# A float32 encoder on one Trainium2 core: the six split-weight buffers at six addresses modulo 256 bytes

## The chip, the core and the metric

The kernel runs on one core of one Trainium2 chip. The metric is the device time of one execution in microseconds (us). Everything is float32; each matrix product is computed from operands that are split into a high and a low part, so one product becomes three matrix instructions.

## What is computed

Two layers of a streaming encoder over 512 frames of width 1024 (batch 1), and a final norm. Cut to what matters here:

```python
h = rmsnorm(x, norm1_g[i])
z = h @ w_in[i] + b_in[i]                  # 1024 -> 12296 columns
# branch A: 4-head mLSTM on conv + silu of q, k; branch B: 4-head retention on rotary q, k
merged = sigmoid(gm) * (y_m @ w_bm[i]) + sigmoid(gr) * (y_r @ w_br[i])
x = x + merged @ w_out[i]
h2 = rmsnorm(x, norm2_g[i])
x = x + square(relu(h2 @ w_ff1[i] + b_ff1[i])) @ w_ff2[i] + b_ff2[i]
h3 = rmsnorm(x, norm3_g[i])
x = x + sigmoid(h3 @ w_pe_gate[i]) * (p[i] @ w_pe[i])
...
return rmsnorm(x, final_g)
```

## The kernel before

Activations lie transposed in the core's memory (features in the 128 partitions, 512 frames along the row), weights come from device memory in the order of a list of units. A **unit** is a 1024 x 128 column block (T8: eight 128 x 128 pieces), a value block (V), a PAIR (two such column blocks, multiplied by a seven-product scheme with halves of the operands) or a WIDE (the same scheme with 512 weight columns moving). For every 1024-column piece of a unit, `prep_next` takes the raw tile `wr` that a load on SP's queue has filled and splits it: ScalarE copies it rounded into `wh` (L303), VectorE subtracts and writes the rest into `wl` (L304). TensorE then runs, for each 128 x 128 piece, three instructions: weight high x activation high, weight high x activation low, weight low x activation high (`mm3`, L480 to L482; in pairs L531 to L533 with 256 columns moving; in WIDE units L575 to L577, where a piece of the activation sits still and 512 weight columns move). GpSimd's queue adds weight pieces in device memory ahead of time for the seven-product scheme (L361).

TensorE's work is written out in program order, and VectorE's and ScalarE's splits are held in the order of the units. `unit` and `ready` keep the splits two pieces ahead of TensorE; six buffers of 1024 columns (tag "w", three pieces of a high and a low tile) and two of 512 columns (tag "d") hold the split weights. The pools stand one behind the other from the low end of the 128 rows: constants, columns, a filler of 48 floats (`pad`), the weight pool (`wr` four buffers, "w" six, "d" two), then the tiles that live through the kernel, then pools that come and go by phase, on the left (low addresses) or on the right (from the top).

All sizes but the small ones are multiples of 256 bytes, so what decides an address modulo 256 is the filler and a small tile named `shift`. In the program before, every weight buffer, raw or split, starts at 224 modulo 256. So do all the activation tiles that TensorE reads, but for three groups that a `shift` tile of 16 floats moves to 32: the operand sums of the seven-product scheme in the first half of a layer (`xsh`, `xsl`), the hidden tiles of the feed-forward (`hh`, `hl`) and the embedding input (`pth`, `ptl`). The operands `xnh`, `xnl`, `ymh`, `yrh`, `n2h`, `nsh`, `nsl` and the like are at 224.

```python
    def shift(pl, side, start):

        if (side == "left") == start:
            pl.tile([P, 16 if start else 48], F32, name="shift", tag="shift")
```

Of the kernel before, what the change touches and what calls it, by code (L numbers as in the profile page):

```python
# [35 lines left out]
F32 = mybir.dt.float32  # L36
F32R = mybir.dt.float32r
# [5 lines left out]
P = 128  # L43
# [4 lines left out]
L = 2  # L48
# [8 lines left out]
NTMP = 6  # L57
RAWS = 4
PIECES = 3
PAD = 48  # L60
LAST = 4
SIGN = (1.0, -1.0)

# [60 lines left out]
def is_wide(g):  # L124
    return g[1][:2] in ("rv", "rw")
# [7 lines left out]
def has_t2(g):  # L133

    return is_full(g) or g[1][0] == "f"
# [117 lines left out]
def build(ctx, tc, ins, out):  # L253
# [3 lines left out]
    NU = len(units)  # L257

    def pool(name, bufs, **kw):
        return ctx.enter_context(tc.tile_pool(name=name, bufs=bufs, **kw))  # L260
# [3 lines left out]

    cpool = pool("const", 1)
    cols = pool("cols", 2)
    padp = pool("pad", 1)
    padp.tile([P, PAD], F32, name="pad")
    wpool = pool("w", PIECES)
    bpool = pool("big", 1)  # L270
    opool = pool("one", 1)
# [30 lines left out]
    def split(src, hi_ap, lo_ap):  # L302
        a = ac.activation(hi_ap, src, AF.Copy)  # L303
        return a, ve.tensor_sub(lo_ap, src, hi_ap.bitcast(F32))  # L304

    def in_order(kind, *new):

        for a, b in zip(cur.get(kind, ()), new):
            tc.add_manual_dep(b.ins, a.ins.name, ORDER, reason="order of the weights")
        cur[kind] = new  # L310
# [4 lines left out]
    for g, v in groups().items():  # L315
        index[g] = len(index)
        src, n, w = ("wwide", 2, UN) if is_wide(g) else ("wpairs", len(v), Q)
# [63 lines left out]
    def full(n):  # L381
        return units[n][0] in ("PAIR", "WIDE") and is_full(units[n][1])
# [10 lines left out]
    def halves(n):  # L393

        return [slice(0, Q), slice(Q, UN)] if n == 1 else [slice(0, UN)]

    def fill_raws(most=RAWS + 1):
        while at["load"] < len(loads) and len(raws) + len(kept) < most:
            n, x = loads[at["load"]]
            r = None  # L400
            if n in cur["room"] and cur["more"] not in raws:
                cur["more"] = n, x
                r = cur["low"].tile([P, UN], F32, name=f"wr{at['load']}", tag="wrx", bufs=1)
            elif len(raws) - (cur["more"] in raws) >= RAWS:
                break
            raws[n, x] = r = r or wpool.tile([P, UN], F32, name=f"wr{at['load']}", tag="wr", bufs=RAWS)
            if x:
                _, g, p = units[n]
                assert made.get((g, x[1] if is_wide(g) else p)) == 2 * len(MADE_OF(g)), (g, p, made, at["unit"])
                if is_wide(g):  # L410
                    in_order("load", nc.sync.dma_start(r, block(g, x[0])[x[1]]))
                else:
                    for k, y in enumerate(PIECE[x][:1] if x == "B" and not has_t2(g) else PIECE[x]):
                        in_order("load", nc.sync.dma_start(r[:, k * Q:(k + 1) * Q], block(g, y)[p]))
            elif units[n][0] == "IF":
                eng = nc.sync if n else nc.scalar
                eng.dma_start(r[:, 0:64], ins["wif"][n * L // NU])
            else:
                w = ins["wstream"][at["whole"]]
                for c in halves(n):  # L420
                    in_order("load", nc.sync.dma_start(r[:, c], w[:, c]))
                at["whole"] += 1
            at["load"] += 1

    def prep_next():
        n, x = order[at["prep"]]
        at["prep"] += 1
        fill_raws()

        w = Q if x == "D" else UN  # L430
        pl = cur["last"] if n >= NU - LAST else wpool
        kw = {"tag": "d", "bufs": 2} if x == "D" else {"tag": "l", "bufs": 2 * LAST} if pl is not wpool else {
            "tag": "w", "bufs": 2 * PIECES}
        wide = isinstance(x, tuple)
        nm = f"{x[0]}{x[1]}" if wide else x
        gates = units[n][0] == "IF"
        out_ = [pl.tile([P, w], F32R, name=f"w{a}{n}_{nm}", **kw) for a in ("h" if gates else "hl")]
        r = formed.pop((n, x), None)
        if r is None:
            r = raws.pop((n, x))  # L440
        if gates:
            z = out_[0]
            gp.memset(z.bitcast(F32), 0.0)
            z = z.rearrange("p (k g c) -> p k g c", g=4, c=32)
            split(r[:, 0:64].rearrange("p (k g c) -> p k g c", g=2, c=H), z[:, :, 0:2, 0:H], z[:, :, 2:4, 0:H])
        elif x == 0:
            with tc.high_priority(AHEAD if n < 10 and units[n][0] == "V" or units[n][1:] == SOON else 0):
                for c in halves(n):
                    in_order("prep", *split(r[:, c], *[a[:, c] for a in out_]))
        else:  # L450
            in_order("prep", *split(r[:, :w], *out_))
        pieces[n, x] = out_
        if full(n) or not wide and x in ("A", "C") and has_t2(units[n][1]):
            pass
        elif x == "A" or wide and x[0] == "t2":
            kept[n, x] = r
        elif x == "C":

            ve.tensor_tensor(raws[n, "B"][:, Q:], kept.pop((n, "A"))[:, Q:], r[:, :Q], OP.add)
        elif x == "B":  # L460

            ve.tensor_tensor(r[:, :Q], r[:, :Q], r[:, Q:], OP.add)  # L462
            formed[n, "D"] = r
        elif wide and x[0] == "B21":
            t = cur["br"].tile([P, UN], F32, name=f"t4{n}_{x[1]}", tag=("ph", "pl")[x[1]])
            ve.tensor_tensor(t, kept.pop((n, ("t2", x[1]))), r, OP.add)
            formed[n, ("t4", x[1])] = t

    def ready(k):
        while at["prep"] < min(len(order), k + 1):  # L470
            prep_next()

    def unit(kind):
        n = next_unit()
        assert units[n][0] == kind, (units[n], kind)
        ready(place[n, 0] + LOOK)
        return units[n], *pieces.pop((n, 0))
# [497 lines left out]
    for i in range(L):  # L975
# [34 lines left out]
        _, wi = unit("IF")  # L1010
        _, wh, wl = unit("T8")
        og = ps(f"l{i}if")
        oz = ps(f"l{i}m0z0")
        for k in range(KT):
            s = slice(k * P, (k + 1) * P)
            f, e = k == 0, k == KT - 1
# [281 lines left out]
        for d in range(4):  # L1298
# [8 lines left out]
            a = (f"l{i}m0{d}", 8 * (d // 2) + d % 2, qk[2 * (d // 2)][d % 2], qk[2 * (d // 2) + 1][d % 2], d < 2, n1)  # L1307
# [347 lines left out]
    for a, n in enumerate(nn):  # L1655
        for c in range(KT - LAST, KT):
            _, wh, wl = ws[c - KT + LAST]
# [143 lines left out]
```

## Time and profile before

| what | value |
|---|---|
| time, median of 2 runs | 2318.26 us (2317.53 to 2318.99) |
| span of the profiled execution | 2313.4 us, first to last instruction |
| outside the span, by the median | 4.9 us |
| TensorE matmul busy | 2299.1 us (99%), 13532 instructions |
| TensorE weight load busy | 2035.4 us (88%) |
| VectorE, ScalarE, GpSimd busy | 1766.8, 1269.6, 624.1 us |
| mean granted TensorE clock | 0.998 |

A row of the timeline gives the start in us, the duration in us, the engine (PE is TensorE, DVE VectorE, ACT ScalarE, POOL GpSimd), the line, the operation, output<-inputs, and the shape. A matmul's duration contains its way through the array and overlaps the next one, so its cost in a stream is the distance from its start to the next start. PEld is TensorE loading the next 128 x 128 piece that sits still, beside the running matmul.

### The profile page before, as it was taken

Reading aid. Unit: us, or ns where it says so; the run is one execution under the profiler, and the core shown is the slowest. Engines: PE = TensorE matmul, PEld = TensorE weight load, DVE = VectorE, ACT = ScalarE, POOL = GpSimd, SP = SyncE. Lnnn points to the kernel's source line nnn. Section 1 sums busy time; section 2 is a strip of 40 time slices with the busy share of each in tenths; the row PEclk is TensorE's granted clock in tenths of the full one; section 3 lists DMA queues with packets and bytes.
Section 4 is the critical chain, followed back from the end, with each engine's and each line's share of the span. In section 5 each row is a group of like instructions: output and inputs, shape, how many; then the busy total and the mean of one; then the engine's idle time right before and its main releaser. Section 6 shows DMA issues by size and latency. Waiting matters only on the chain.

```text
span 2313.4 us, 36468 instructions
## 1 busy us (share of the span) xinstructions
PE 2299.1 (99%) x13532; PEld 2035.4 (88%) x13532; DVE 1766.8 (76%) x2690; ACT 1269.6 (55%) x1837; POOL 624.1 (27%) x984
## 2 busy tenths in 40 slices
PE   9999999999999999999999999999999999999998
PEld 8888899888898899999888888988888888999997
DVE  7878767886676878788778777778867678787785
ACT  6756544644554546556557564445445446566564
POOL 4333222223124322223442332221231242111112
PEclk9999999999999999999999999999999999999999
DMA  7776787777789888888886768877877898878851
GB/s 218 189 191 174 238 228 216 215 227 210 232 230 261 220 228 223 240 239 215 222 224 182 196 174 247 232 216 216 223 221 208 241 266 218 247 232 228 232 160 55
DMA packets 187603, 499.36 MB, mean 216 GB/s; under 512 B 26064, under 2 KB 29520, under 8 KB 187424
## 3 DMA queue, kind: packets, MB, share of 16 engines
q0 software_dynamic: 57520, 188.53, 37.1%
q1 hardware_dynamic: 114496, 281.06, 36.6%
q10 hardware_dynamic: 15408, 27.43, 3.5%
q8 instruction: 106, 1.74, 0.3%
q14 instruction: 73, 0.60, 0.1%
HBM read 478.05 MB, written 194.51 MB: 291 GB/s over the span
## 4 chain that ended last, share of the span: by engine, by line
PE 92%; DVE 5%; ACT 1%; issue 1%; DMA 1%; POOL 0%; SPq 0%; ACTq 0%; DVEq 0%; POOLq 0%
PE l0br L480 1%; PE l1br L480 1%; PE l1br L481 1%; PE l0br L482 1%; PE l1br L482 1%; PE l0br L481 1%; PE l0f L480 1%; PE l0f L481 1%; PE l0f L482 1%; PE l1f L480 1%; PE l1f L481 1%; PE l1f L482 1%; PE l0pg L480 1%; PE l1bm L480 1%; PE l0pg L482 1%
## 5 line engine op out<-in xcount | busy, mean ns | idle before, releaser
L303 ACT ACTIVATE wh<-wr 128x1024 fp32r<-128x1024 f32 (+1 forms) x193 | 199.7, 1041 | 140.5 <-issue 17.1
L304 DVE TENSOR_TENSOR wl<-wr,wh 128x1024 fp32r<-128x1024 f32 (+1 forms) x191 | 234.6, 1230 | 37.5 <-ACT wh L303 36.9
L303 ACT ACTIVATE wh_B<-wr 128x1024 fp32r<-128x1024 f32 x123 | 130.3, 1059 | 184.5 <-PE l0br L481 15.7
L304 DVE TENSOR_TENSOR wl_B<-wr,wh_B 128x1024 fp32r<-128x1024 f32 x123 | 150.3, 1222 | 55.1 <-ACT wh_B L303 50.6
L303 ACT ACTIVATE wh_C<-wr 128x1024 fp32r<-128x1024 f32 x75 | 79.2, 1056 | 69.5 <-PE l0br L481 8.3
L304 DVE TENSOR_TENSOR wl_C<-wr,wh_C 128x1024 fp32r<-128x1024 f32 x75 | 91.7, 1223 | 21.3 <-ACT wh_C L303 17.1
L303 ACT ACTIVATE wh_A<-wr 128x1024 fp32r<-128x1024 f32 x75 | 78.9, 1052 | 44.3 <-DMA wr<-wpairs 5.2
L304 DVE TENSOR_TENSOR wl_A<-wr,wh_A 128x1024 fp32r<-128x1024 f32 x75 | 91.6, 1221 | 12.6 <-ACT wh_A L303 9.4
L303 ACT ACTIVATE wh_D<-wr 128x512 fp32r<-128x512 f32 x75 | 47.2, 630 | 96.5 <-DVE wr L462 27.3
L303 ACT ACTIVATE wh_t<-wr 128x1024 fp32r<-128x1024 f32 x56 | 59.4, 1061 | 69.0 <-PE l0g2va L576 6.0
L304 DVE TENSOR_TENSOR wl_t<-wr,wh_t 128x1024 fp32r<-128x1024 f32 x56 | 68.2, 1221 | 26.1 <-ACT wh_t L303 25.5
L304 DVE TENSOR_TENSOR wl_D<-wr,wh_D 128x512 fp32r<-128x512 f32 x75 | 51.8, 690 | 30.2 <-ACT wh_D L303 28.7
L480 PE MATMUL l0f<-l0n2h,wh 128*128 128x512 f32 x176 | 68.7, 390 | 0.0
L481 PE MATMUL l0f<-l0n2l,wh 128*128 128x512 f32 x176 | 68.6, 390 | 0.0
L482 PE MATMUL l0f<-l0n2h,wl 128*128 128x512 f32 x176 | 68.5, 389 | 0.0
L361 POOL DMA_DIRECT2D s30t<-wpairs x24 | 16.8, 699 | 92.4 <-PE l1o11a L533 9.4
L482 PEld LDWEIGHTS l0f<-l0n2h,wl 128*128 128x128 f32 x176 | 33.0, 188 | 7.0
L480 PEld LDWEIGHTS l0f<-l0n2h,wh 128*128 128x128 f32 x176 | 33.1, 188 | 6.6
L481 PEld LDWEIGHTS l0f<-l0n2l,wh 128*128 128x128 f32 x176 | 33.1, 188 | 6.5
L480 PE MATMUL l1f<-l1n2h,wh 128*128 128x512 f32 x96 | 37.6, 391 | 0.0
L481 PE MATMUL l1f<-l1n2l,wh 128*128 128x512 f32 x96 | 37.5, 390 | 0.0
L482 PE MATMUL l1f<-l1n2h,wl 128*128 128x512 f32 x96 | 37.4, 389 | 0.0
(5797 smaller groups left out, 9132.4 us busy)
## 6 DMA issues: line engine op xcount, KB each, us to landing
wr<-wstream SPq DMA_DIRECT2D x189, 512.0 KB, 4.8
wr<-wpairs SPq DMA_DIRECT2D x225, 256.0 KB, 4.1
wr<-wwide SPq DMA_DIRECT2D x48, 512.0 KB, 4.7
s3t<-wwide POOLq DMA_DIRECT2D x24, 256.0 KB, 5.0
s6t<-wwide POOLq DMA_DIRECT2D x24, 256.0 KB, 5.0
s18t<-wwide POOLq DMA_DIRECT2D x24, 256.0 KB, 4.7
s21t<-wwide POOLq DMA_DIRECT2D x24, 256.0 KB, 5.3
s24t<-wpairs POOLq DMA_DIRECT2D x24, 256.0 KB, 5.7
```

What stands on the lines that cost most here:

```text
L303: a = ac.activation(hi_ap, src, AF.Copy)
L304: return a, ve.tensor_sub(lo_ap, src, hi_ap.bitcast(F32))
L361: dma = gp.dma_start(piece(g, x, p, q), piece(g, MADE[x][a], p, q), max_dma_last_dim=4096, **kw)
L480: te.matmul(o, sh, mh, start=first, stop=False)
L481: te.matmul(o, sh, ml, start=False, stop=False)
L482: cur["mm"] = te.matmul(o, sl, mh, start=False, stop=last)
```

## The change

The filler goes. Each buffer of the weight pool's tags "w" and "d" becomes 8 floats (32 bytes) longer, and the tile is a window of the old width in it: at its start in the first layer, 4 floats (16 bytes) further in the second. Raw tiles keep their size, and the tiles of the last four units, which come from another pool, are as before.

```diff
-PAD = 48
+SKEW = 8
...
-    padp = pool("pad", 1)
-    padp.tile([P, PAD], F32, name="pad")
     wpool = pool("w", PIECES)
...
         gates = units[n][0] == "IF"
-        out_ = [pl.tile([P, w], F32R, name=f"w{a}{n}_{nm}", **kw) for a in ("h" if gates else "hl")]
+        skew = SKEW if pl is wpool else 0
+        at_ = skew // 2 * (n * L // NU)
+        out_ = [pl.tile([P, w + skew], F32R, name=f"w{a}{n}_{nm}", **kw)[:, at_:at_ + w] for a in ("h" if gates else "hl")]
```

The layout that follows, as starts modulo 256 bytes:

| tiles | before | after, layer 0 | after, layer 1 |
|---|---|---|---|
| raw weights `wr` | 224 | 32 | 32 |
| six split buffers | 224 | 32, 64, 96, 128, 160, 192 | 48, 80, 112, 144, 176, 208 |
| two split buffers of 512 columns | 224 | 224, 0 | 240, 16 |
| tiles behind the weight pool on the left | 224 (shifted: 32) | 32 (shifted: 96) | 32 (shifted: 96) |
| tiles on the right | 224 (shifted: 32) | the same | the same |

On the left lie in the first layer `xn`, `ym`, `yr`, `hh`, `hl` and in the second `xs`, `n2`, `nsl`; on the right lie in the first layer `xs`, `n2`, `ns` and in the second `xnl`, `ym`, `yr`, `hh`, `hl`. The high halves `xnh`, and in the second layer `nsh`, stand directly behind the weight pool and move like the left ones. The order of instructions on each of the five engines' queues is the same row for row; no instruction is added, removed or moved.

## The prediction

> **What bounds the kernel.** I read the page's busy shares first, then its slices, then the chain that ended last.
>
> ```profile
> PE 2299.1 (99%) x13532; PEld 2035.4 (88%) x13532; DVE 1766.8 (76%) x2690; ACT 1269.6 (55%) x1837; POOL 624.1 (27%) x984
> PEclk9999999999999999999999999999999999999999
> DMA  7776787777789888888886768877877898878851
> PE 92%; DVE 5%; ACT 1%; issue 1%; DMA 1%; POOL 0%; SPq 0%; ACTq 0%; DVEq 0%; POOLq 0%
> ```
>
> The matmul rows cover 2299.1 us of a span of 2313.4, the granted clock is high in all slices, and the chain runs through PE for 92% of the span. So PE is idle for only 14.3 us. The change adds no instruction and moves none; it can alter the time only by altering how long existing work takes. The question is therefore what one matmul costs in the stream, and whether that depends on addresses. The table of costly groups does not say it, since its durations overlap. I went to the timeline, and took pairs of rows that stand exactly 24 matmuls apart.
>
> First, 512 columns moving, three kinds of operands:
>
> ```profile
> 286.36 0.39 PE L480 MATMUL l0bm<-l0ymh,wh 128*128 128x512 f32 x1
> ...
> 291.80 0.39 PE L480 MATMUL l0bm<-l0ymh,wh 128*128 128x512 f32 x1
> ```
> ```profile
> 2202.07 0.40 PE L480 MATMUL l1pe<-l1pth,wh 128*128 128x512 f32 x1
> ...
> 2207.58 0.28 PE L531 MATMUL l1o30a<-l1hh,wh_A 128*128 128x256 f32 x1
> ```
> ```profile
> 250.07 0.40 PE L575 MATMUL l0r0vc<-wh_t,l0xsh 128*128 128x512 f32 x1
> ...
> 255.67 0.40 PE L575 MATMUL l0r0va<-wh_t,l0xsh 128*128 128x512 f32 x1
> ```
>
> In the first pair the moving operand `ymh` and the weights both start at 224 modulo 256: 5.44 us / 24 = **226.7 ns** each. In the second the moving operand is at 32 and the weights at 224 (moving minus still: 64): 5.51 / 24 = **229.6**. In the third the weights move at 224 and `xsh` sits still at 32 (moving minus still: 192): 5.60 / 24 = **233.3**. The same number of columns and the same clock, and three prices.
>
> Now 256 columns moving:
>
> ```profile
> 2115.49 0.28 PE L531 MATMUL l1f23b<-l1n2h,wh_B 128*128 128x256 f32 x1
> ...
> 2118.37 0.28 PE L531 MATMUL l1f23a<-l1nsh,wh_C 128*128 128x256 f32 x1
> ```
> ```profile
> 2165.34 0.28 PE L531 MATMUL l1o23b<-l1hh,wh_B 128*128 128x256 f32 x1
> ...
> 2168.17 0.28 PE L531 MATMUL l1o23a<-l1hh,wh_C 128*128 128x256 f32 x1
> ```
> ```profile
> 1989.53 0.28 PE L531 MATMUL l1o02c<-l1hh,wh_A 128*128 128x256 f32 x1
> ...
> 1992.25 0.28 PE L531 MATMUL l1o02a<-l1hh,wh_B 128*128 128x256 f32 x1
> ```
>
> With difference 0 it is 2.88 / 24 = **120.0 ns**. With difference 64 it is 2.83 / 24 = **117.9** in one stretch and 2.72 / 24 = **113.3** in another, with the same kind of tiles at the same residues. 113.3 is half of 226.7, so I take 0.4427 ns per column as the price without disturbance, 6.7 ns as what difference 0 costs a short matmul, and 6.6 as what difference 192 costs a long one. That one pair of residues has two prices tells the reader something else: it is not the difference alone, but also where the two streams stand against each other when a series begins.
>
> Which two streams? The windows over two such stretches show it:
>
> ```profile
> 286.30:297.30 11.00, 11.00 (x50) 9.09 (x50) 6.53 (x8) 2.76 (x3) 3.48 (x5) 1.00 0.89 242
> 2116.90:2122.65 5.75, 5.75 (x50) 5.75 (x49) 5.61 (x9) 3.44 (x5) 1.00 (x2) 1.00 0.84 296
> ```
>
> The columns are the length, then busy time of PE, PEld, DVE, ACT, POOL, then clock and DMA. With 512 columns the weight load covers 9.09 of 11.00 us, with 256 columns all of 5.75. A short matmul has a load beside it from its start to its end, a long one has slack. The load rows themselves lengthen with the residue:
>
> ```profile
> L531 PEld LDWEIGHTS l0r0brqa<-l0xnh,wh_A x4: 188/192/192, 305.9 to 307.0; 128*128 128x128 f32 x4
> L531 PEld LDWEIGHTS l0r0brqc<-l0xsh,wh_A x4: 187/188/192, 307.4 to 308.5; 128*128 128x128 f32 x4
> ```
>
> Minimum, median and maximum: 192 ns in the median with the moving operand at the same residue, 188 with 64 between them. So I read the extra nanoseconds as the moving stream and the load of the next still piece getting in each other's way, by addresses modulo 256. This is a reading, not yet a test.
>
> The Trainium skill speaks against this reading, and so against any effect of the change. Its page "SBUF — State Buffer", section "Who interferes with whom", gives TensorE two independent read ports and says that TensorE never waits on anyone; its page "TensorE: Matmul & The Clock Gate", section "Step-by-step: what each phase is for", says that loading the next weights takes no read bandwidth from the running matmul. By that rule the sum below would be 0. The trace disagrees, with 120.0, 117.9 and 113.3 ns for one shape.
>
> **The change part by part.** Counted in the program by operands and their residues, the matmuls are: 2268 of 256 columns in pairs at difference 0; 4032 of 256 columns in pairs at difference 64; 4976 of 512 columns at difference 0 (T8 units, value units, the WIDE products on `xn`); 768 of 512 columns at difference 192 (the WIDE products on `xs`); 96 of the embedding; 192 of 256 columns at difference 0 in the last four units. The rest, some 870 of the two recurrences, has no weight buffer in it and keeps its residues.
>
> *What the skew does.* In layer 0 the differences become all eight multiples of 32, in layer 1 all eight of these plus 16, about evenly. Fewer than 500 of the 12,332 counted keep their old value. The three matmuls of one piece use the high buffer twice and the low buffer once, so within a unit the difference alternates between two values, and the next unit has another two. The trace shows no row for such a series.
>
> *Bounds.* From below: every pair matmul comes to 113.3 (2268 x 6.7 + 4032 x 4.6 = 33.7 us), every WIDE product on `xs` to 226.7 (768 x 6.6 = 5.1), and small change (the 192 matmuls of the last units, which get difference 64: at most 1.3; the embedding 0.3): -40 us. From above: pairs all at 120.0 (4032 x 2.1 = 8.5) and the long matmuls all at 233.3 (4976 x 6.6 = 32.8): +41 us. Dearer than every row seen is possible, cheaper than 113.3 and 226.7 is not to be expected, since half the columns cost half.
>
> *The value I take.* With many differences mixed, no row is nearer than another, so I take the mean of the three rows of each size: (113.3 + 117.9 + 120.0) / 3 = 117.1 and (226.7 + 229.6 + 233.3) / 3 = 229.9. Pairs at difference 0: 2268 x (117.1 - 120.0) = -6.6. Pairs at 64: 4032 x (117.1 - 117.9) = -3.2. Long ones at 0: 4976 x (229.9 - 226.7) = +15.9. WIDE on `xs`: 768 x (229.9 - 233.3) = -2.6. Last units: -0.4. Sum: **+3 us**. The asymmetry is the point of the whole case. The short matmuls have now something to gain, the long ones sit at their best price and can only lose, and there are thousands of each.
>
> *The filler, the raw tiles, the tiles on the left.* Removing 192 bytes and adding six times 32 leaves the space behind the six buffers where it was; the two smaller buffers then move everything on the left by 64 bytes. That is in the differences above. For the other engines the sum has nothing:
>
> ```profile
> L303 ACT ACTIVATE wh_B<-wr 128x1024 fp32r<-128x1024 f32 x123 | 130.3, 1059 | 184.5 <-PE l0br L481 15.7
> L304 DVE TENSOR_TENSOR wl_B<-wr,wh_B 128x1024 fp32r<-128x1024 f32 x123 | 150.3, 1222 | 55.1 <-ACT wh_B L303 50.6
> wr<-wpairs SPq DMA_DIRECT2D x225, 256.0 KB, 4.1
> ```
>
> A split costs 1059 ns on ACT and 1222 on DVE per 1024 columns whichever buffer it goes to, and a pair unit (84 matmuls at 117.9 = 9.9 us) needs three and a half of them, 4.3 us of DVE. If other residues made a split 5% slower, that is 0.2 us per pair, under cover of PE and of the two pieces that the splits run ahead; bound: nothing, unless DVE (76% busy) becomes the end of a unit, which these 5% don't do. The loads land in 4.1 us in the median and are issued up to four tiles ahead. If the best case came, a pair would take 9.5 us and the cover would still hold: of 40 us gained, perhaps 2 come back as waits, by the 14.3 us of idle time that PE has in the whole span.
>
> **The sum.** The profiled span of 2313.4 and 4.9 us around it give the median of 2318.3. Plus 3: **2321 us**, a difference that nobody would see, since 2% (46 us) is what a measurement of this kernel can tell from no change.
>
> **Rivals.**
> 1. *The streams no longer meet* (chance 0.22). With another residue on every buffer the load may fall into the gaps of the moving stream, as in the stretch at 1989.53. For it: 113.3 exists at an unchanged pair of residues. Against it: the stretch is rare; the other feed-forward products with the same tiles stand at 117.9. Whole price -40: 2278; half of it: 2298.
> 2. *The long matmuls lose their quiet state* (0.23). Place: T8 units, L480 to L482. At difference 0 they run at 226.7 for long series; with two alternating differences they would never settle, and stand at 233.3 as the WIDE products on `xs` do. Price 4976 x 6.6 = 32.8, with all pairs at 117.9 (2268 x 2.1 = 4.8 gained): +28, 2346; with all pairs at 120.0, 2360. It decides against all gains of the pairs (33.7) as soon as the long ones cost 6.8 ns more each; over 2% it needs 9.3 more, 236.0 each, beyond the rows.
> 3. *Addresses do nothing* (0.10), and the prices come from something else in these stages: 2318. For it: two prices at one pair of residues. Against it: PEld at 192 and 188 within 1.5 us of each other, as the products alternate between `xnh` and `xsh`.
>
> The forecast, a mixture with both signs, has 0.45.
>
> **How the numbers follow.** The forecast's own range is 2307 to 2333 (half of each size's swing). Taking in half of rival 1 and most of the way to rival 2's 2346, the range is 2292 to 2345; what is left out is the full price of either, 2 in 10. Faster than 2272 would need more than the -40 of the bound: 0.02. Slower than 2364.6 needs prices above all rows: 0.05. The rest, 0.93, is within 2%.
>
> **What will show it.** In the profile after, rows 24 apart: T8 units at 226.7 mean rival 2 is wrong, near 233 that it is right; pair products at 113.3 mean rival 1. Differences between layer 0 and layer 1 in the same product would show what the 16 bytes are worth. PEld medians of 188 against 192 go with the short matmuls. Wrong at the root is the prediction if DVE or ACT splits change by more than 5%, if PE's idle time leaves the 14 us, or if one matmul price goes outside 113 to 120 or 226 to 234.

## The result and the profile after

| | before | after |
|---|---|---|
| time, median of 2 runs each | 2318.26 us | 2339.91 us (2339.34 to 2340.48) |
| ratio | 1 | 1.0098, 95% interval 1.0079 to 1.0117 |
| span of the profiled execution | 2313.4 us | 2337.6 us |

The change costs 21.7 us, where +3 was forecast: slower by 1%, inside the range of 2292 to 2345 and near its upper end. The page of the changed kernel, with busy shares, granted clock by slices and the chain that ended last:

```profile
PE 2321.8 (99%) x13532; PEld 2037.5 (87%) x13532; DVE 1768.6 (76%) x2690; ACT 1271.2 (54%) x1837; POOL 622.9 (27%) x984
PEclk9999999999999999999999999999999999999999
PE 92%; DVE 3%; issue 2%; DMA 1%; ACT 1%; POOL 1%; ACTq 0%; DVEq 0%; POOLq 0%
```

The counts of instructions are the same, and the mean clock is 0.998 in both. PE's busy time rises by 22.7 us and the span by 24.2; time without PE goes from 14.3 to 15.8. (By the spans the change costs 2.5 us more than by the times: 1.7 us lie outside the span after and 4.9 before, so the profiled execution of before was shorter than the timed ones by some 3 us, an estimate from these two.) So it is the price of a matmul, and hardly a wait. The splits, as groups with busy time and mean ns, are what they were (1059 and 1222 ns before):

```profile
L301 ACT ACTIVATE wh_B<-wr 128x1024 fp32r<-128x1024 f32 x123 | 130.4, 1060 | 191.7 <-PE l0br L481 16.4
L302 DVE TENSOR_TENSOR wl_B<-wr,wh_B 128x1024 fp32r<-128x1024 f32 x123 | 150.3, 1222 | 55.8 <-ACT wh_B L301 55.4
```

Now the timeline of the changed kernel, in the way the prediction read it: rows 24 matmuls apart (48 apart for `l0wo`), start in us first.

```profile
288.63 0.40 PE L480 MATMUL l0bm<-l0ymh,wh 128*128 128x512 f32 x1
...
294.23 0.39 PE L480 MATMUL l0bm<-l0ymh,wh 128*128 128x512 f32 x1
...
733.97 0.40 PE L480 MATMUL l0wo<-l0mh,wh 128*128 128x512 f32 x1
...
745.14 0.39 PE L480 MATMUL l0wo<-l0mh,wh 128*128 128x512 f32 x1
```
```profile
2138.99 0.28 PE L531 MATMUL l1f23b<-l1n2h,wh_B 128*128 128x256 f32 x1
...
2141.83 0.28 PE L531 MATMUL l1f23a<-l1nsh,wh_C 128*128 128x256 f32 x1
...
2189.21 0.28 PE L531 MATMUL l1o23b<-l1hh,wh_B 128*128 128x256 f32 x1
...
2192.03 0.28 PE L531 MATMUL l1o23a<-l1hh,wh_C 128*128 128x256 f32 x1
```

The T8 unit `l0bm` takes 5.60 us / 24 = 233.3 ns a matmul, where the same operands took 226.7; `l0wo` takes 11.17 / 48 = 232.7. The pair product at 2138.99 takes 118.3 and was 120.0; the one on the hidden tiles takes 117.5 and was 117.9. In these rows the long matmuls lost some 6 ns each, and the short ones won less than 2.

Over all start-to-start distances of a class in the two traces, the 24.2 us between the spans are as follows. Distances over 133 ns (256 columns) and over 249 ns (512 columns) are counted as late starts.

| class | mean before | mean after | sum, worked out |
|---|---|---|---|
| 512 columns at difference 0 (T8, V, WIDE on `xn`) | 227.3 ns | 231.9 ns | +22.6 us |
| 256 columns at difference 0, last units included | 119.9 | 118.4 | -3.5 us |
| 256 columns at difference 64 | 117.3 | 118.3 | +4.0 us |
| WIDE on `xs` | 233.3 | 232.1 | -0.9 us |
| embedding | 229.6 | 232.0 | +0.2 us |
| late starts | | | +1.1 us |
| the 1200 matmuls without a weight buffer | | | +0.6 us |

The classes are named by their difference before, and the sums are worked out before rounding. They come to 24.1 us, against 24.2 between the spans. Late starts are no part of the story: 58 short matmuls start late in either trace. But 115 short ones stand at 129 to 132 ns after the change, 91 of them in the first layer, where none stood before in either layer; they belong to the price.

### The profile page after: what moved, and what is told of

Same layout as the page of the kernel before. It is cut to its first block, busy times and chain, and to the rows that moved or that the text cites. A ratio compares the mean times of both kernels' runs of the same rounds, so it can differ in the third digit from the quotient of the medians.

```text
span 2337.6 us, 36468 instructions
## 1 busy us (share of the span) xinstructions
PE 2321.8 (99%) x13532; PEld 2037.5 (87%) x13532; DVE 1768.6 (76%) x2690; ACT 1271.2 (54%) x1837; POOL 622.9 (27%) x984
## 4 chain that ended last, share of the span: by engine, by line
PE 92%; DVE 3%; issue 2%; DMA 1%; ACT 1%; POOL 1%; ACTq 0%; DVEq 0%; POOLq 0%
PE l0f L481 2%; PE l0f L480 2%; PE l0f L482 2%; PE l0br L481 1%; PE l0br L480 1%; PE l0br L482 1%; PE l1br L482 1%; PE l1br L481 1%; PE l1br L480 1%; PE l1f L480 1%; PE l1f L482 1%; PE l1f L481 1%; PE l0bm L481 1%; PE l0pg L480 1%; PE l0wo L481 1%
## 5 line engine op out<-in xcount | busy, mean ns | idle before, releaser
L301 ACT ACTIVATE wh_B<-wr 128x1024 fp32r<-128x1024 f32 x123 | 130.4, 1060 | 191.7 <-PE l0br L481 16.4
L302 DVE TENSOR_TENSOR wl_B<-wr,wh_B 128x1024 fp32r<-128x1024 f32 x123 | 150.3, 1222 | 55.8 <-ACT wh_B L301 55.4
L302 DVE TENSOR_TENSOR wl_C<-wr,wh_C 128x1024 fp32r<-128x1024 f32 x75 | 91.7, 1222 | 20.5 <-ACT wh_C L301 19.6
L302 DVE TENSOR_TENSOR wl_A<-wr,wh_A 128x1024 fp32r<-128x1024 f32 x75 | 91.6, 1222 | 12.8 <-ACT wh_A L301 11.3
L301 ACT ACTIVATE wh_t<-wr 128x1024 fp32r<-128x1024 f32 x56 | 59.3, 1060 | 69.5 <-PE l1g2va L576 6.0
L302 DVE TENSOR_TENSOR wl_t<-wr,wh_t 128x1024 fp32r<-128x1024 f32 x56 | 68.3, 1222 | 26.4 <-ACT wh_t L301 25.8
L480 PE MATMUL l0f<-l0n2h,wh 128*128 128x512 f32 x176 | 69.5, 395 | 0.0
L482 PE MATMUL l0f<-l0n2h,wl 128*128 128x512 f32 x176 | 69.3, 394 | 0.0
L482 PEld LDWEIGHTS l0f<-l0n2h,wl 128*128 128x128 f32 x176 | 33.1, 188 | 7.8
L480 PEld LDWEIGHTS l0f<-l0n2h,wh 128*128 128x128 f32 x176 | 33.0, 188 | 7.6
L480 PE MATMUL l1f<-l1n2h,wh 128*128 128x512 f32 x96 | 38.0, 396 | 0.0
L482 PE MATMUL l1f<-l1n2h,wl 128*128 128x512 f32 x96 | 37.9, 394 | 0.0
```

Of the source, the lines that this page charges most:

```text
L480: te.matmul(o, sh, mh, start=first, stop=False)
L482: cur["mm"] = te.matmul(o, sl, mh, start=False, stop=last)
```

## The experiments

Two theories were set against each other. **A**: a matmul's price is set by the value of the difference, moving minus still, modulo 256 bytes, and difference 0 is simply cheap for the long ones. **B**: a value costs nothing by itself; what costs is that in the changed kernel the difference alternates within a series.

### One offset for all weight buffers

These four kernels keep the kernel before, but move all weight buffers, raw and split, by the same 32, 64, 128 or 192 bytes, and put everything behind them back. No difference alternates within a product.

```diff
-PAD = 48
+PAD = 64
...
     wpool = pool("w", PIECES)
+    padq = pool("padq", 1)
+    padq.tile([P, 48], F32, name="padq")
```

That is the edit for 64 bytes; for 32, 128 and 192 the two numbers are 56 and 56, 80 and 32, 96 and 16.

> The same with 32 bytes: long matmuls and the first pairs at difference 224, the pairs on shifted operands at 32. Theory A: another price again for each, long matmuls over 228; B: long matmuls near 227, total within 10 us of before.

> All weight buffers, raw and split, start 64 bytes further (32 modulo 256 instead of 224), the tiles behind them stay where they were: the difference moving minus still is one constant for each kind of operand. Long matmuls at difference 0 get 192, pairs at 0 get 192, pairs at 64 get 0. Theory A (the price hangs on the value of the difference): long matmuls 233 ns, pairs on the shifted operands 120.0; about +33 +8 us, some 2355 us. Theory B (the price in the changed kernel comes from a difference that alternates within a series, a constant one settles): long matmuls stay near 227, total within 10 us of before.

> The same with 128 bytes: long matmuls and the first pairs at difference 128, the pairs on shifted operands at 192. Theory A: long matmuls near the changed kernel's 232 ns, +25 us or more, some 2345 us; theory B: near 227, total within 10 us of before.

> The same with 192 bytes: long matmuls and the first pairs at difference 64, the pairs on shifted operands at 128. Theory A: long matmuls at the embedding's 229.6 ns, +14 us, first pairs 117.9, -5 us; some 2328 us plus what 128 does to 4032 pairs. Theory B: within 10 us of before, below it by the 5 us of the first pairs.

Measured, one run each, beside 2317.48 us of the kernel before: 2342.61 (32 bytes), 2334.34 (64), 2330.42 (128), 2328.89 (192). All are slower by 11 to 25 us, though within a product nothing alternates: B's "within 10 us of before" fails four times. A's 2328 for 192 bytes is met; its 2355 and 2345 for 64 and 128 bytes were 21 and 15 us too high. They left out the short matmuls that come to difference 192 and get cheaper (114.2 and 115.4 ns in the mean). The one for 64 bytes also took value units and WIDE products on `xn` to be at 192; there the weights are the moving operand, so the difference is 64, and they cost 230. The timelines of the kernels with 64 and with 128 bytes, 24 matmuls apart:

```profile
288.51 0.39 PE L482 MATMUL l0bm<-l0ymh,wh 128*128 128x512 f32 x1
...
294.11 0.39 PE L482 MATMUL l0bm<-l0ymh,wh 128*128 128x512 f32 x1
...
2129.89 0.28 PE L533 MATMUL l1f23a<-l1n2h,wh_A 128*128 128x256 f32 x1
...
2132.62 0.28 PE L533 MATMUL l1f23a<-l1nsh,wh_B 128*128 128x256 f32 x1
```
```profile
288.56 0.39 PE L482 MATMUL l0bm<-l0ymh,wh 128*128 128x512 f32 x1
...
294.13 0.39 PE L482 MATMUL l0bm<-l0ymh,wh 128*128 128x512 f32 x1
...
2174.84 0.28 PE L533 MATMUL l1o23a<-l1hh,wh_A 128*128 128x256 f32 x1
...
2177.56 0.28 PE L533 MATMUL l1o22a<-l1hh,wh_D 128*128 128x256 f32 x1
```

With the weights at 32 (difference 192) `l0bm` takes 233.3 ns, the price that the prediction read from the WIDE products, and the pair product falls from 120 to 113.8. With difference 128 (the second fence) `l0bm` takes 232.1, and the pair on the hidden tiles, now at 192, takes 113.3. So a constant difference has a price of its own, and it is another one for long and short. The Trainium skill's page "SBUF — State Buffer", section "Who interferes with whom", says that TensorE never waits on anyone. These four runs, the same instructions at other addresses between 2329 and 2343 us, disagree if the extra time is a wait; whether it is one, they don't show.

### Only the activations moved

If it is the difference that counts, and not where the weights lie, then moving the other operand must do the same. The shifted groups (`xs`, hidden tiles, embedding input) go from 32 to 160, and the weights stay at 224.

```diff
-            pl.tile([P, 16 if start else 48], F32, name="shift", tag="shift")
+            pl.tile([P, 48 if start else 16], F32, name="shift", tag="shift")
```

> The kernel before with the weights where they were (224), and the shifted activations (operand sums xs, hidden tiles, embedding input) at 160 instead of 32. Theory A, the difference decides: 4032 pair matmuls go from difference 64 to 192 (117.2 to 114.6 ns, -10.5 us), 768 WIDE ones on xs from 192 to 64 (233.2 to 229.4, -2.9), 96 of the embedding +0.4: 12 us less, 2306. Theory C, the weights' own address decides (all constant offsets so far moved the weights): nothing changes, 2318.

Measured over 5 runs: **2305.85 us, ratio to before 0.9945 (0.9931 to 0.9958)**. A's 2306 is met. PE's row and a pair product on the hidden tiles, 24 matmuls apart, in this kernel:

```profile
PE 2287.5 (99%) x13532; PEld 2027.1 (88%) x13532; DVE 1764.4 (77%) x2690; ACT 1270.0 (55%) x1837; POOL 624.6 (27%) x984
```
```profile
2155.57 0.28 PE L531 MATMUL l1o23b<-l1hh,wh_B 128*128 128x256 f32 x1
...
2158.29 0.28 PE L531 MATMUL l1o23a<-l1hh,wh_C 128*128 128x256 f32 x1
```

PE's busy time is 11.6 us below that of before, and the product that stood at 117.9 ns stands at 113.3 (in the mean of 4010 such matmuls 115.1). This is the opposite of the edit studied: it gives most short matmuls their best difference and leaves the long ones at theirs. It beats both kernels.

### The two values that were missing

The first layer of the changed kernel has all eight multiples of 32. Differences 96 and 160 had not been seen; the same `shift` tile gives them.

```diff
-            pl.tile([P, 16 if start else 48], F32, name="shift", tag="shift")
+            pl.tile([P, 40 if start else 24], F32, name="shift", tag="shift")
```

> The kernel before with the shifted activations at 128: pair products on xs and on the hidden tiles have difference 160, WIDE ones on xs 96, two values that the first layer of the changed kernel has and no constant offset has shown so far. By neighbours in the table of constant differences (short: 128 118.7, 192 114.6; long: 64 229.4, 128 232.6) I expect short ones at 116 to 118 and long ones at 230 to 232: -7 to +1 us, 2311 to 2319. If the price were the same at every constant difference other than 0 (a theory that the WIDE ones at 229.4 and 233.2 already speak against), pairs stay at 117.2 and the time at 2318.

With the numbers 24 and 40 instead:

> The kernel before with the shifted activations at 64: pair products on xs and on the hidden tiles at difference 96, WIDE ones on xs at 160. By neighbours (short: 64 116.9, 128 118.7; long: 128 232.6, 192 233.3) short ones at 117 to 119, long ones at 232 to 234: -1 to +8 us, 2317 to 2326.

Measured beside 2317.33: 2320.35 and 2323.65. The short ones stand at 118.2 (difference 160) and 119.9 (96), the long ones at 233.3 (96) and 234.1 (160). The prices were expected between those of the neighbours, and that was wrong three times out of four (the first total, 2320.35, lies outside its 2311 to 2319 too): 96 is dear although 64 is cheaper, in both sizes. These are the rows for the long ones, WIDE products on `xs`, at difference 96 and then, from the other kernel, at 160:

```profile
249.93 0.39 PE L575 MATMUL l0r0vc<-wh_t,l0xsh 128*128 128x512 f32 x1
...
255.53 0.39 PE L575 MATMUL l0r0va<-wh_t,l0xsh 128*128 128x512 f32 x1
```
```profile
249.81 0.39 PE L575 MATMUL l0r0vc<-wh_t,l0xsh 128*128 128x512 f32 x1
...
255.43 0.40 PE L575 MATMUL l0r0va<-wh_t,l0xsh 128*128 128x512 f32 x1
```

5.60 / 24 = 233.3 and 5.62 / 24 = 234.2 ns. Now the price list by constant difference is complete in steps of 32. Each number is the mean start-to-start distance of that class in one trace, with the count of matmuls:

| difference | 256 columns, ns | 512 columns, ns |
|---|---|---|
| 0 | 119.9 (2421, kernel before) | 227.3 (3951, kernel before) |
| 32 | 117.1 (4010, offset 32) | 233.3 (948, offset 32) |
| 64 | 117.3 (4010, kernel before) | 229.2 (3939, offset 192) |
| 96 | 119.9 (4010, shift 24) | 233.3 (758, shift 40) |
| 128 | 118.9 (2233, offset 128) | 232.7 (3945, offset 128) |
| 160 | 118.2 (4010, shift 40) | 234.1 (762, shift 24) |
| 192 | 114.3 (2232, offset 64) | 233.3 (3939, offset 64) |
| 224 | 118.2 (2232, offset 32) | 233.2 (3939, offset 32) |
| mean of the eight | **118.0** | **232.1** |

For 512 columns one value is good, one fair, six are bad. Several kernels give the same difference to other tiles, and in value units and WIDE products the roles are exchanged (the weights move); the means still agree within some 2 ns. At 192, 256 columns have 114.2, 115.1 and 115.4; at 64, 512 columns have 229.0, 229.2, 229.3, 230.0 and 230.2. An even spread over all eight gives the last row, and that is nearly what the changed kernel shows: 118.3 and 231.9. Its second layer, though, has differences 16 bytes off these eight, and for those no run gives a price at a constant difference.

### High and low halves at two addresses

Alternation by itself: three buffers of one ring (buffers that are handed out in turn) for the high halves at 224, three of a second ring for the low halves at 32, and everything else at its old residue. Two of the three matmuls of a piece keep their difference.

```diff
 PAD = 48
+GAPS = {"wl": 16}
+BEHIND = 48
...
     wpool = pool("w", PIECES)
+    padq = pool("padq", 1)
+    padq.tile([P, BEHIND], F32, name="padq")
...
+        def half(a):
...
+            tag = kw["tag"] + a
+            if GAPS.get(tag) and tag not in cur:
+                wpool.tile([P, GAPS[tag]], F32, name="gap" + tag, tag="gap" + tag, bufs=1)
...
-        out_ = [pl.tile([P, w], F32R, name=f"w{a}{n}_{nm}", **kw) for a in ("h" if gates else "hl")]
+        out_ = [half(a) for a in ("h" if gates else "hl")]
```

> The kernel before, but each low half of the split weights stands 64 bytes further modulo 256 than its high half (high 224, low 32; the two small buffers both at 32), everything else at its old residue. Within a unit the difference moving minus still now alternates: 0, 0, 192 for the long matmuls on operands at 224, 64, 64, 0 for the pair products on operands at 32. Theory A (each matmul has the price of its own difference, whatever its neighbours have): long matmuls (2 x 227.3 + 233.3) / 3 = 229.3 ns, short ones 117.9 in the mean; +6 us, about 2324. A matmul at difference 0 still takes about 227 and 120 ns. Theory B (a series with alternating differences never settles, and loses the cheap price everywhere): long matmuls at 231.5 to 233 also where their own difference is 0; +19 to +25 us, about 2337 to 2343, like the changed kernel.

Measured: 2337.7 us, B's number, but not for B's reason alone. Late starts add 5.6 us over the trace of before (18.8 against 13.2), mostly where TensorE now waits for a split, which it didn't in the kernel before. Three such waits, with engine and line, what was waited for, and us in total, times and longest:

```profile
PE l1r2vc L591 <- ACT wh_t L308: 0.9, 1, 0.9
PE l1r2vc L592 <- DVE wl_t L309: 0.8, 1, 0.8
PE l0r2vc L592 <- DVE wl_t L309: 0.8, 1, 0.8
```

The rest is price. The timeline, 24 matmuls apart:

```profile
288.20 0.40 PE L496 MATMUL l0bm<-l0ymh,wh 128*128 128x512 f32 x1
...
293.76 0.39 PE L496 MATMUL l0bm<-l0ymh,wh 128*128 128x512 f32 x1
```

`l0bm` takes 5.56 / 24 = 231.7 ns, and all T8 units 231.1 in the mean, where the price list gives (2 x 227.3 + 233.3) / 3 = 229.3. By position in the piece, the three matmuls take 228.9, 229.5 and 234.9 (some 1300 of each): the two with difference 0 do not get the 227.3 that a quiet series has, nor do they rise to B's 231.5 to 233. So A is not the whole: what precedes a matmul counts too. B holds as an addition for the long ones; the short ones, 117.2 and 118.0 ns, are at or under the list (118.0 and 118.2).

The WIDE products suggest what it is that precedes. On `xs` the weights move at 224, 32, 224 over a still piece at 32, so that the matmul's own difference is 192, 0, 192. The three take 235.3, 237.0 and 230.2 ns (248, 252 and 227 of them): the one at difference 0 is the dearest. Set what moved in the matmul before against the piece that sits still now, and the differences are 192, 192, 0, in the order of the prices. These two streams run at the same time: in the timeline each piece loads (PEld) while the matmul before it runs, as here on `xn`.

```profile
250.47 0.40 PE L592 MATMUL l0r0va<-wl_B,l0xnh 128*128 128x512 f32 x1
250.47 0.19 PEld L593 LDWEIGHTS l0r0va<-wh_B,l0xnl 128*128 128x128 f32 x1
250.70 0.40 PE L593 MATMUL l0r0va<-wh_B,l0xnl 128*128 128x512 f32 x1
```

Where the still operand alone alternates, as in T8 units, the two ways of counting give the same. This is one kernel and a pattern nobody had foretold, so it favours the prediction's reading and doesn't prove it.

### Alternation from piece to piece only

Here the high and the low half of a piece were to share a residue, with the three pieces at 32, 96 and 160, so that a T8 unit has one difference from its first matmul to its 24th.

```diff
-PAD = 48
+GAPS = {"wl": 16}
+ROOM = 16
...
+            more = ROOM if x != "D" else 0
+            return wpool.tile([P, w + more], F32R, name=f"w{a}{n}_{nm}", tag=tag, bufs=kw["bufs"])[:, 0:w]
```

> High and low half of one piece at the same residue, but the three pieces at three residues (32, 96, 160; the small buffers at 224), operands as before. Within a T8 unit the difference is constant, from unit to unit it goes over 192, 128, 64. Theory A: each class has the price that it had with one offset for all buffers: long at difference 64 229.4, 128 232.6, 192 233.3 ns; short at 0 119.8, 32-multiples as measured (64 116.9, 128 118.7, 192 114.6); sum +17 us, about 2335. Theory B (only a change inside a series costs): the same or less for T8 units, since inside a unit nothing changes, so that B gives about the same total; what tells them apart here is the short products, whose difference changes from one product of a pair to the next, 12 matmuls long: by A they keep the spread of 114.6 to 119.8 by class, by B they come together near 118 as in the changed kernel.

Measured: 2341.2 us, 6 above what the price list gives. Late starts are 7.5 us above those of before, with the same waits for splits among them, and can account for that.

The edit does not do what the expectation says in the first layer. The unit of the gates at the head of each layer takes a high buffer and no low one (`"h" if gates else "hl"`), so the ring of high buffers runs ahead of the ring of low ones, and the halves of a piece lie at two residues. A trace holds no addresses, but the T8 units bear this out. By position in the piece their matmuls take 234.6, 231.3 and 230.7 ns in the first layer, unequal as in the kernel with two addresses, and 231.7, 231.4 and 231.8 in the second, where the gates' second buffer seems to bring the rings together again. There, sorted by the order in which the program hands out the buffers, the long classes are by the list (229.5 at 64, 232.3 at 128, 233.3 at 192). In the first layer 234.6 lies above every price that the list has for the three residues. So the run divides as the kernel with two addresses would have it: matmul by matmul, the list holds where a unit has one difference, and not where it alternates. The residues of the first layer are argued from the code and not measured.

### The 16 bytes, and the tiles on the left

The changed kernel without the second layer's 16 bytes:

```diff
-        at_ = skew // 2 * (n * L // NU)
+        at_ = 0
```

> The changed kernel without the 16 bytes of the second layer: the windows stand at the start of their buffers in both layers. Theory A: in layer 1 the differences become the eight multiples of 32, as in layer 0; the long matmuls of layer 1 rise from 231.4 to layer 0's 232.2 ns (2231 x 0.8 = 2 us) and the rest stays: 2341 to 2343. Theory B (alternation alone costs, not where the differences stand): no change within 1 us, 2340.

Measured: 2337.53 us. The T8 and V matmuls of the second layer go from 231.2 to 231.9 ns, as A expected, but the time doesn't rise, and is 2 us less. With one run, and two of the changed kernel that are 1.1 us apart, this is no difference that I would name. The 16 bytes are worth nothing that shows, and neither theory is decided by it.

The changed kernel with the tiles on the left back at 224:

```diff
     bpool = pool("big", 1)
+    padq = pool("padq", 1)
+    padq.tile([P, 48], F32, name="padq")
```

(The new pool stands ahead of `bpool`.)

> The changed kernel with 48 floats behind the weight pool, so that the tiles on the left, high halves included, are back at 224 (shifted 32); the six skewed buffers and the 16 bytes of layer 1 stay. Theory A (the mean of the differences) and the mixing of theory B both expect long matmuls at 231 to 232 and short ones at 117.6 to 118.3, since every buffer still has another difference: 2336 to 2342, within 4 us of the changed kernel. If it was the move of the left tiles that cost, against the raw tiles or against the tiles on the right that stayed, the time falls back by most of the 22 us, to 2318 to 2325.

Measured: 2339.78 us, the time of the changed kernel. The move of the left tiles costs nothing that shows; the skewed buffers are enough for the whole loss.

## Why the prediction was near and where it failed

- **PE is the bound, and only the price of a matmul can move the time: right.** Busy time of PE is +22.7 of 24.2 us of span, and the clock is the same.
- **Addresses modulo 256 set the price: right**, and now tested: moving the weights (11 to 25 us slower) and moving activations (12 us faster) both come out by the difference. Rival 3, addresses do nothing, was 21.7 us off. So was the 0 that the prediction worked out by the Trainium skill's page "SBUF — State Buffer", section "Who interferes with whom".
- **"With many differences mixed, no row is nearer than another, so I take the mean of the three rows": this step failed.** The three long rows were those at 0, 64 and 192, which are the best, the second best and one of six bad ones. Their mean is 229.9; the mean over eight is 232.1, and the changed kernel has 231.9. The term of the long matmuls was +15.9 and measured +22.6. The cheap price was not one of three, but one of eight.
- **The short ones at difference 64** were given -3.2 and measured +4.0, the other sign. The mean of the rows held 113.3, which was a rare state of difference 64 (some 13% of these matmuls stood at 114 ns or less before) and not a value that a mix reaches; it is the usual price only at 192 (113.3 and 113.8 in the rows above). The mean of eight is 118.0, above the 117.3 that these matmuls had.
- **The short ones at difference 0**: -6.6 forecast, or -7.0 with the last units, and -3.5 measured with them. **WIDE on `xs`**: -2.6 and -0.9. Right in sign, too large for the same reason.
- With the completed price list, the same counts give 2268 x (118.0 - 119.9) = -4.3, 4032 x (118.0 - 117.3) = +2.8, 4976 x (232.1 - 227.3) = +23.9 and 768 x (232.1 - 233.3) = -0.9: +21.5. Taking a mean of prices came out, with eight samples instead of three. That agreement is one of sums, and in part luck: the second layer's differences are not on the list, and in the kernel with two addresses the list falls 1.8 ns short for T8 units. The measured time lies inside the range because the range took in most of rival 2, and not because the sum was near.
- **Rival 2** was the course of things, with its place (T8, L480 to L482) and half of its reason: a series with alternating differences does lose the cheap price, but a constant difference other than 0 loses it as well. It priced 28 to 42 us, with 233.3 ns for each. The series stand at 231.9, and the pairs pay nothing back (+0.5 together). **Rival 1** is refuted as a consequence of this change, but 113.3 is real, and with the `shift` of 48 floats the 4032 come to 115.1 in the mean.
- **The splits under cover of PE: right** (1060 and 1222 ns). PE's idle time outside the rows went to 15.8 us, not out of place. The matmuls without a weight buffer are 1200 (13532 - 12332) and not some 870, which are the products of the recurrences alone; all 1200 cost +0.6 us.
- **"Outside 113 to 120 or 226 to 234"**: the means by class are inside (118.3 to 118.4, 231.9 to 232.1). Single matmuls are not: 115 short ones stand at 129 to 132 ns.
- **"PEld medians of 188 against 192 go with the short matmuls": right.** For the 2268 at difference 0 the median was 192 before, and it is 188 after. With all weights 64 bytes further these have 188, and the 4032 that come to difference 0 have 192. But only the load beside a short matmul at difference 0 is longer: at 96, where a short matmul costs as much (119.9), and beside the long ones at any price the median stays at 188. So the length of a load goes with the stream beside it at difference 0, and does not account for the prices.

## What to carry to other kernels

Where the bound is TensorE and the profile shows a matmul at two prices, list the starts of both operands modulo 256 bytes and price every value of their difference with a uniform offset before spreading buffers over many: here a spread paid about the mean of all values, and a quiet series at the best value was worth more than variety. Long and short matmuls may want different values (here 0 and 192), so give each group of operands its own; moving the operand that only one kind reads costs one small tile. A mean over the rows that a kernel happens to show is a sample chosen by how the kernel was laid out, and should widen the estimate towards the values not seen.

## What the hardware showed that was not expected

- The price is not smooth in the difference: for 512 columns 227.3, 233.3, 229.2, 233.3 ns at 0, 32, 64, 96.
- The two sizes want different values: at 192, 256 columns cost 114.3 ns, their least, and 512 columns 233.3, almost their most.
- One difference has two lasting states. With all weights 192 bytes further, `l0m1z` and `l0bm` both run at difference 64. The timeline of that kernel, 48 matmuls apart for the first and 24 for the second:

```profile
74.04 0.39 PE L482 MATMUL l0m1z<-l0n1h,wh 128*128 128x512 f32 x1
...
85.03 0.39 PE L482 MATMUL l0m1z<-l0n1h,wh 128*128 128x512 f32 x1
...
287.75 0.40 PE L482 MATMUL l0bm<-l0ymh,wh 128*128 128x512 f32 x1
...
293.35 0.40 PE L482 MATMUL l0bm<-l0ymh,wh 128*128 128x512 f32 x1
```

10.99 / 48 = 229.0 and 5.60 / 24 = 233.3 ns. In the first series single distances go round between 226, 229 and 232 ns; in the second all 96 are 233 or 234 but two. `l0bm` follows WIDE products there, and seems to keep the state in which it starts; in the second layer the four units behind the WIDE products stand at 233.3 ns too. What that state is stays open. That the second stream is the load of the next weights, as the prediction read it, is favoured by the loads that lengthen with difference 0 and by the WIDE products of the kernel with two addresses, but not shown: all runs move addresses, and none takes the load away.
